# Four of eight gate/up pieces of each feed-forward chunk in seven block products instead of eight

## The chip, the cores and the metric

The kernel runs on one core of a Trainium2 chip. The metric is the device time of one execution in microseconds (us), from the runs shown; a profiled execution gives the span from its first to its last instruction. The engines are PE (TensorE: matmuls, with PEld for its weight loads), DVE (VectorE), ACT (ScalarE), POOL (GpSimd) and SP (SyncE, which here only issues loads). SBUF is the on-chip memory, PSUM holds matmul sums in eight banks of 128 x 512 fp32 numbers.

## What is computed

A two-layer decoder trunk on 256 tokens of width 2048 in fp32. Layer 0 mixes tokens by a diagonal state-space model with a GLU, layer 1 by sliding-window attention; each is followed by a SwiGLU feed-forward layer of inner width 5632, which is what the change touches:

```
D_MODEL = 2048; SEQ = 256; DEPTH = 2
D_FF = ((8 * D_MODEL // 3 + 255) // 256) * 256        # 5632

def swiglu(x, w_gate, w_up, w_down):
    return (jax.nn.silu(x @ w_gate) * (x @ w_up)) @ w_down

for i in range(DEPTH):
    hn = rmsnorm(h, norm_mix[i])
    ...
    h = h + mix
    hn = rmsnorm(h, norm_ffn[i])
    h = h + swiglu(hn, ffn_w_gate[i], ffn_w_up[i], ffn_w_down[i])
return rmsnorm(h, norm_final)
```

## The kernel before

**Numbers in two halves.** A big matrix product is made in three matmuls per block: each fp32 operand is split into a high half, rounded to the short form fp32r, and a low half, the rest, and the products high x high, high x low and low x high are summed in PSUM (`products`, lines 926 to 928). The activations are the stationary operand (128 x 128), the weights the moving one (128 x 512).

**Weight pieces.** All weights come as pieces of 512 x 512, in one list whose order is the order of use (class `Weights`). SP loads a piece (1 MB) into one of two `raw` buffers (`load`, line 109). ACT copies it into the high half of a tile `w` (`high`, line 122), DVE subtracts that from the raw piece for the low half (`low`, line 127). There are three `w` tiles. `next` (line 134) hands out piece i, splits up to piece i + 2 and loads up to i + 4; a `w` tile comes free when PE has done with the piece three before. A piece takes PE 4 row blocks x 2 token tiles x 3 = 24 matmuls (`piece`, line 930).

**A feed-forward layer** (`swiglu`, line 1128) works in eleven chunks of 512 inner columns. For a chunk, `gu` takes four gate pieces into two banks (one per tile of 128 tokens), four up pieces into two more, forms silu(gate) x up (lines 1152 and 1156), and turns the gated chunk around for use as stationary operand `hT`: 16 transposes of 32 x 256 on DVE (`blocks_turned`, line 1007), then the split by ACT and DVE (lines 1165 and 1166). The last chunk of a layer is turned by PE (line 1137). `down` multiplies `hT` with the down weights and adds to the residual `h` (line 1177), in four column blocks. The groups of chunks are `((0, 1, 2), (3, 4, 5), (6, 7, 8), (9, 10))`; the down product of a group comes after the first chunk of the next group (`ffn_order`, line 166). Four `hT` tiles (`b8`) exist.

**Small work in between.** Steps that turn and split are put into the list `left` and popped piece by piece in `linear` (line 941), so that they are written between the pieces' matmuls. In the norm ahead of a feed-forward layer (`Norm`, line 1010, with `blocks`) the residual is turned in the same way and split with the norm's weight as a scale (lines 1036 and 1037); the row scale of the norm is applied after the products. Another way of turning is used for the norm ahead of the attention (`through`): one DVE transpose of 32 x 32 blocks (line 1045), then POOL moves the blocks through DRAM (`through_dram`, lines 998 and 999), then the split (lines 1055 and 1060).

**Order.** The kernel is written in a tile language: it decides itself in which order ready instructions stand on an engine and puts in all waits; a tile of a pool with n buffers waits for the release of the one n before. Only where `keep_in_program_order` is used does the written order hold.

## Time and profile before

| | |
|---|---|
| time, median of 3 runs | 1981.72 us (1980.31 to 1982.71) |
| span of the profiled execution | 1976.9 us |
| HBM read / written | 363.72 MB / 8.91 MB |
| mean TensorE clock granted | 0.993 |
| pieces of weights | 332 (11 x 8 gate/up and 44 down pieces per feed-forward layer) |
| L926, L927, L928 with `xT`, `hT`, `gt` as stationary operand | 3 x 2528 matmuls, 390 ns each, overlapping |
| q1 (SP's loads) | 356.87 MB, 56.4% of 16 DMA engines |

The lines of the profile read: source line, engine, operation, tile written from tiles read, shapes and count, then the busy time in us, the mean duration in ns, and the idle time of the engine ahead of them with what ended it. In a timeline a line begins with the start and the duration in us, and ends with the idle time before it in brackets. In a table of stretches each engine has its busy time and the number of its instructions, in the order PE, PEld, DVE, ACT, POOL; then follow the granted clock, the share of the DMA engines' time and GB/s.

### The profile page before, as it was taken

The page shows a single profiled execution, that of the slowest core. Times are in us where ns is not written, and L with a number is a line of the kernel's source. Part 1 is how long each engine was busy: PE and PEld are TensorE (multiplying, and loading weights), DVE is VectorE, ACT ScalarE, POOL GpSimd, SP SyncE. Part 2 cuts the span into 40 slices and gives each one's busy share as a digit, 9 for nine tenths or more (in the row PEclk, how much of TensorE's full clock was granted, in tenths as well). Part 3 has the DMA queues.
Part 4 walks back from the last instruction along what each step waited for, and adds up shares of the span by engine and source line. Part 5 has one row for each costly group of instructions (what it writes and reads, how often), then busy time and mean ns, then how long its engine had stood idle before and what let it go on. Part 6 is the DMA issues. An engine that isn't in the chain of part 4 may idle for free.

```text
span 1976.9 us, 24861 instructions
## 1 busy us (share of the span) xinstructions
PE 1935.3 (98%) x10312; PEld 1600.9 (81%) x10312; DVE 1287.2 (65%) x1689; ACT 859.9 (43%) x839; POOL 130.5 (7%) x122
## 2 busy tenths in 40 slices
PE   8699999999999999999999999999999999999998
PEld 6578888888888888888888778888888888888886
DVE  8966667666556656665577888766654665566545
ACT  6554444343334333433455554443333434333333
POOL 6850000000000000000010110000000000000000
PEclk9899999999999999999999999999999999999999
DMA  4037666556666665656585864665566556656664
GB/s 131 24 103 224 209 207 199 182 186 209 192 192 188 195 197 186 201 189 205 176 280 186 261 226 150 195 209 192 191 192 192 191 191 201 195 190 188 205 191 149
DMA packets 188181, 374.23 MB, mean 189 GB/s; under 512 B 11203, under 2 KB 11267, under 8 KB 187941
## 3 DMA queue, kind: packets, MB, share of 16 engines
q1 hardware_dynamic: 183168, 356.87, 56.4%
q0 software_dynamic: 4064, 13.65, 2.1%
q10 hardware_dynamic: 836, 2.14, 0.3%
q8 instruction: 80, 1.31, 0.3%
q14 instruction: 33, 0.26, 0.0%
HBM read 363.72 MB, written 8.91 MB: 188 GB/s over the span
## 4 chain that ended last, share of the span: by engine, by line
PE 91%; DVE 6%; DMA 1%; issue 1%; ACT 1%; POOL 0%; DVEq 0%; POOLq 0%; ACTq 0%
PE acc L926 30%; PE acc L927 29%; PE acc L928 29%; DVE scan L577 1%; DVE V L582 1%; DVE V L580 1%; DVE w L127 1%; PE pv L214 1%; PE py L802 0%; DMA pT<-pd 0%; DMA pd<-bt 0%; PE px L214 0%; DVE bt L1285 0%; DMA raw<-in_attn_w_qkv_dram 0%; ACT w L122 0%
## 5 line engine op out<-in xcount | busy, mean ns | idle before, releaser
L127 DVE TENSOR_TENSOR w<-raw,w 128x2048 fp32r<-128x2048 f32 x330 | 756.9, 2294 | 579.4 <-ACT w L122 577.4
L122 ACT ACTIVATE w<-raw 128x2048 fp32r<-128x2048 f32 x332 | 636.1, 1916 | 840.6 <-PE acc L928 543.1
L926 PE MATMUL acc<-w,xT 128*128 128x512 f32 x1568 | 611.8, 390 | 0.0
L928 PE MATMUL acc<-w,xT 128*128 128x512 f32 x1568 | 611.0, 390 | 0.0
L927 PE MATMUL acc<-w,xT 128*128 128x512 f32 x1568 | 610.9, 390 | 0.0
L926 PEld LDWEIGHTS acc<-w,xT 128*128 128x128 f32 x1568 | 294.5, 188 | 62.4 <-issue 1.8
L928 PEld LDWEIGHTS acc<-w,xT 128*128 128x128 f32 x1568 | 294.5, 188 | 61.4 <-issue 0.3
L927 PEld LDWEIGHTS acc<-w,xT 128*128 128x128 f32 x1568 | 294.5, 188 | 60.7
L926 PE MATMUL acc<-w,hT 128*128 128x512 f32 x704 | 274.6, 390 | 0.0
L927 PE MATMUL acc<-w,hT 128*128 128x512 f32 x704 | 273.9, 390 | 0.0
L928 PE MATMUL acc<-w,hT 128*128 128x512 f32 x704 | 273.6, 390 | 0.0
L926 PEld LDWEIGHTS acc<-w,hT 128*128 128x128 f32 x704 | 132.2, 188 | 28.3 <-ACT hT L1139 1.2
L928 PEld LDWEIGHTS acc<-w,hT 128*128 128x128 f32 x704 | 132.2, 188 | 27.5
L927 PEld LDWEIGHTS acc<-w,hT 128*128 128x128 f32 x704 | 132.2, 188 | 27.2
L1007 DVE STREAM_TRANSPOSE bt<-act 32x256 f32<-32x256 f32 x320 | 139.6, 436 | 5.5
L927 PE MATMUL acc<-w,gt 128*128 128x512 f32 x256 | 99.9, 390 | 0.6 <-DVE w L127 0.6
L926 PE MATMUL acc<-w,gt 128*128 128x512 f32 x256 | 100.0, 391 | 0.0
L928 PE MATMUL acc<-w,gt 128*128 128x512 f32 x256 | 99.8, 390 | 0.0
L998 POOL DMA_DIRECT2D pd<-bt x40 | 21.9, 553 | 932.9 <-DVE bt L1045 842.7
L1165 ACT ACTIVATE hT<-bt 128x1024 fp32r<-128x1024 f32 x20 | 21.2, 1062 | 96.9 <-DVE bt L1007 96.8
L1007 DVE STREAM_TRANSPOSE bt<-h 32x256 f32<-32x256 f32 x128 | 55.8, 436 | 1.9
L1177 DVE TENSOR_TENSOR h<-h,acc 128x512 f32<-128x512 f32 x64 | 43.0, 686 | 21.4 <-PE acc L928 21.4
(249 smaller groups left out, 1283.3 us busy)
## 6 DMA issues: line engine op xcount, KB each, us to landing
raw<-in_ffn_w_gate_dram SPq DMA_DIRECT2D x88, 1024.0 KB, 5.2
raw<-in_ffn_w_up_dram SPq DMA_DIRECT2D x88, 1024.0 KB, 5.2
raw<-in_ffn_w_down_dram SPq DMA_DIRECT2D x88, 1024.0 KB, 5.1
raw<-in_s_w_glu_dram SPq DMA_DIRECT2D x32, 1024.0 KB, 5.4
raw<-in_attn_w_qkv_dram SPq DMA_DIRECT2D x20, 1024.0 KB, 5.2
raw<-in_attn_w_o_dram SPq DMA_DIRECT2D x16, 1024.0 KB, 5.2
pd<-bt POOLq DMA_DIRECT2D x24, 192.0 KB, 4.7
pT<-pd POOLq DMA_DIRECT2D x6, 768.0 KB, 5.8
```

The lines of the kernel that those rows point to most:

```text
L122: keep(S.activation(w[:, 0], self.raw[i], AF.Copy))
L127: keep(e.tensor_tensor(lo, self.raw[i], hi.bitcast(F32), op=ALU.subtract))
L214: return (lambda *a, **k: pin(f(*a, **k))) if self.on else f
L577: keep(V.tensor_tensor(t_, ws[..., part], bc(Vt[hf][:, k - 1, :, part], 1, 2), op=ALU.mult))
L580: V.tensor_tensor(v, v, t_[:, 0], op=ALU.add)
L926: keep(PE.matmul(acc, x_[:, 0], w[0][:, a], start=first, stop=False))
L927: PE.matmul(acc, x_[:, 0], w[1][:, a], start=False, stop=False)
L928: PE.matmul(acc, x_[:, 1], w[0][:, a], start=False, stop=last)
L998: nc.gpsimd.dma_start(d[t].rearrange("(q k) e -> k q e", q=4), v[32 * t : 32 * t + 32])
L1007: V.transpose(dst[32 * q : 32 * q + 32, :, :, 32 * tb : 32 * tb + 32], src[:, :, :, 32 * q : 32 * q + 32])
L1165: S.activation(o[:, 0], v, AF.Copy)
L1177: V.tensor_tensor(hc, hc, acc[t], op=ALU.add)
```

## The change

**Seven products.** Of the eight gate/up pieces of a chunk four (`SEVEN`) are made by Strassen's scheme in Winograd's form. A gate/up piece is now 256 rows of the up and the gate weights side by side, 2 x 2 blocks of 128 x 512: two row blocks by up/gate. The activations' counterpart is 2 x 2 blocks, two token tiles by the same two row blocks. The eight block products of such a pair become seven, of sums and differences of blocks. The products of all four pieces are summed in seven banks, and the four results are put together from them at the end of the last (`sums`, and the additions of `c11` to `c22`). The other four pieces are made in eight products as before, into the same banks and an eighth, `c22`.

**Forms of the operands.** `sevenths` makes a weight piece ready: DVE forms four differences `f` from the raw piece, ACT and DVE split them into the tile `w`, and split the three blocks used as they are into a second tile `d`, of which there is one. `forms` does the same for the activations of two of the four row blocks in a norm chunk.

**Order.** The chunks are in groups of two (the last of three), and half of the previous group's down pieces follow each chunk from the third on. The gated chunk is turned through DRAM (`moved`) instead of by 16 DVE transposes; the last chunk too. The first six down pieces of the last group use the first two chunks of it first (`LAST_ORDER`). The last part of the attention's output product is moved out of the attention's pool, so that the new tiles can have its space.

```diff
-FF_GROUPS = ((0, 1, 2), (3, 4, 5), (6, 7, 8), (9, 10))
+FF_GROUPS = ((0, 1), (2, 3), (4, 5), (6, 7), (8, 9, 10))
+SEVEN = (0, 2, 4, 6)
...
-                nc.sync.dma_start(t, self.src[i].rearrange("(a p) n -> p a n", p=P))
+                aps, _ = self.src[i]
+                t = pp.tile([P, 4, 512], F32, tag="raw", name=nm("raw"), bufs=2)
+                v = t.rearrange("p (k s) n -> p s k n", s=len(aps))
+                for s, ap in enumerate(aps):
+                    nc.sync.dma_start(v[:, s], ap.rearrange("(a p) n -> p a n", p=P))
...
+        def sevenths(self, i):
+            self.load(i + 1)
+            r = self.raw[i]
+            w = self.place(i)
+            d = self.pool.tile([P, 2, 3, 512], F32R, tag="sd", name=nm("sd"), bufs=1)
+            f = self.pool.tile([P, 4, 512], F32, tag="sf", name=nm("sf"), bufs=1)
+            V.tensor_tensor(f[:, 0:2], bc(r[:, 0], 1, 2), r[:, 1:3], op=ALU.subtract)
+            V.tensor_tensor(f[:, 2], r[:, 2], f[:, 0], op=ALU.subtract)
+            V.tensor_tensor(f[:, 3], r[:, 3], f[:, 2], op=ALU.subtract)
+            S.activation(w[:, 0], f, AF.Copy)
+            S.activation(d[:, 0], r[:, 1:4], AF.Copy)
+            V.tensor_tensor(w[:, 1], f, w[:, 0].bitcast(F32), op=ALU.subtract)
+            V.tensor_tensor(d[:, 1], r[:, 1:4], d[:, 0].bitcast(F32), op=ALU.subtract)
+            pairs = [(d[:, 0, j], d[:, 1, j]) for j in range(3)] + [(w[:, 0, j], w[:, 1, j]) for j in range(4)]
+            self.hl.append(dict(zip(("b11", "b22", "b21", "t1", "t3", "t2", "t4"), pairs)))
...
+    LAST_ORDER = [(n, c) for cs in (FF_GROUPS[-1][:-1], FF_GROUPS[-1][-1:]) for n in (0, 1) for c in cs]
...
+            for p in range(8):
+                W.add(*(w[i, 256 * p : 256 * (p + 1), 512 * c : 512 * (c + 1)] for w in (w_up, w_gate)),
+                      seven=p in SEVEN)
...
+    def ffn_order(gu, down, last):
         for g, chunks in enumerate(FF_GROUPS):
-            for n, c in enumerate(chunks):
+            for j, c in enumerate(chunks):
                 gu(c)
-                if n == 0 and g > 0:
-                    down(g - 1)
-        down(len(FF_GROUPS) - 1)
+                if g > 0 and j < 2:
+                    down(g - 1, (2 * j, 2 * j + 1))
+        last()
...
+    def moved(src):
+        v, land = block_tile(), wp.tile([P, 2, 512], F32, tag="act", name=nm("act"), bufs=2)
+        V.transpose(v.rearrange("p a t -> p (a t)").rearrange("p (q t a k) -> p t a q k", q=4, t=2, a=4),
+                    src.rearrange("p t (a q k) -> p t a q k", a=4, q=4))
+        through_dram(land.rearrange("p t c -> p (t c)").rearrange("p (b e) -> p b e", b=4),
+                     v.rearrange("p a t -> p (a t)").rearrange("p (q e) -> p q e", q=4))
...
+        def forms(self, n, o, v):
+            gc = gcol[:, self.g, 4 * n : 4 * n + 4]
+            g0, g1 = gc[:, 0:1], gc[:, 1:2]
+            hi = o[:, 1024:1920].rearrange("p (f t) -> p f t", f=7)
+            lo = W.pool.tile([P, 7, P], F32R, tag="xs", name=nm("xs"), bufs=4)
+            f = W.pool.tile([P, 7, P], F32, tag="xf", name=nm("xf"), bufs=1)
+            S.activation(f[:, 0], v[:, 0, :P], AF.Copy, scale=g0)
+            S.activation(f[:, 1:3].rearrange("p f t -> p (f t)"), v[:, 1], AF.Copy, scale=g1)
+            V.scalar_tensor_tensor(f[:, 3], v[:, 0, P:], g0, f[:, 2], ALU.mult, ALU.add)
+            V.scalar_tensor_tensor(f[:, 5], v[:, 0, P:], g0, f[:, 0], ALU.mult, ALU.subtract)
+            V.tensor_tensor(f[:, 4], f[:, 3], f[:, 0], op=ALU.subtract)
+            V.tensor_tensor(f[:, 6], f[:, 1], f[:, 4], op=ALU.subtract)
+            S.activation(hi, f, AF.Copy)
+            V.tensor_tensor(lo, f, hi.bitcast(F32), op=ALU.subtract)
+            names = ("a11", "a12", "a22", "s1", "s2", "s3", "s4")
...
+        def three(acc, x_, w, first, last):
+            PE.matmul(acc, x_[0], w[0], start=first, stop=False)
+            PE.matmul(acc, x_[0], w[1], start=False, stop=False)
+            PE.matmul(acc, x_[1], w[0], start=False, stop=last)
+
+        M = {"m1": ("a11", "b11"), "c11": ("a12", "b21"), "c12": ("s4", "b22"), "c21": ("a22", "t4"),
+             "m5": ("s1", "t1"), "m6": ("s2", "t2"), "m7": ("s3", "t3")}
+        FIRST = ("m1", "m6", "m7", "m5", "c11", "c21", "c12")
+        REST = ("m1", "c11", "c12", "m5", "m7", "m6", "c21")
+
+        def gu(c):
+            acc = {}
+            u = W.pool.tile([P, 4, 512], F32, tag="u", name=nm("u"), bufs=1)
+
+            def sums():
+                S.copy(u[:, 0], acc["m1"])
+                V.tensor_tensor(u[:, 1], u[:, 0], acc["m6"], op=ALU.add)
+                V.tensor_tensor(u[:, 2], u[:, 1], acc["m7"], op=ALU.add)
+                V.tensor_tensor(u[:, 1], u[:, 1], acc["m5"], op=ALU.add)
+                V.tensor_tensor(u[:, 3], u[:, 2], acc["m5"], op=ALU.add)
+
+            for p in range(8):
+                w = W.next()
+                forms, e = norm.xt[p // 2]
+                if p in SEVEN:
+                    for m in FIRST if p == 0 else REST:
+                        if p == 0:
+                            acc[m] = bank([P, 512], "acc")
+                        x_, b = M[m]
+                        three(acc[m], forms[x_], w[b], p == 0, m[0] == "m" and p == SEVEN[-1])
+                else:
...
+                if p == SEVEN[-1]:
+                    sums()
+                pop_left((6 if c == 0 else 7) - p)
+            if c == 0:
+                r[0] = norm.scale()
+            sg = wp.tile([P, 2, 512], F32, tag="act", name=nm("act"), bufs=2)
+            for t, (g, m) in enumerate(((0, "c11"), (2, "c21"))):
+                V.tensor_tensor(u[:, g], u[:, g], acc[m], op=ALU.add)
+                S.activation(sg[:, t], u[:, g], AF.Silu, scale=r[0][:, t : t + 1])
+            for t, (g, m) in enumerate(((1, "c12"), (3, "c22"))):
+                V.tensor_tensor(u[:, g], u[:, g], acc[m], op=ALU.add)
+                V.scalar_tensor_tensor(sg[:, t], u[:, g], r[0][:, t : t + 1], sg[:, t], ALU.mult, ALU.mult)
             o = turned_tile("hT")
+            ht[c] = o
+
+            def send():
+                lv = moved(sg)
+
+                def split():
+                    for t in range(2):
+                        hi, lo = (o[:, i, :, t * P : t * P + P].rearrange("p a (b k) -> p a b k", b=4)
+                                  for i in range(2))
+                        v = lv[:, :, t].rearrange("p b a k -> p a b k")
+                        S.activation(hi, v, AF.Copy)
+                        V.tensor_tensor(lo, v, hi.bitcast(F32), op=ALU.subtract)
+
+                left.extend([lambda: None] * 2 + [split])
+
+            left.append(send)
...
+        def last():
+            accs = [[bank([P, 512], "acc") for _ in range(2)] for _ in range(2)]
+            for i, (n, c) in enumerate(LAST_ORDER):
+                piece(accs[n], ht[c], c == FF_GROUPS[-1][0], c == FF_GROUPS[-1][-1])
+                pop_left(3 - i)
+            for n in range(2):
+                add(n, accs[n], True)
+            down(len(FF_GROUPS) - 1, (2, 3))
```

In what the diff leaves out, the pieces that are not in `SEVEN` run as two row blocks x (gate, up) x two token tiles, three matmuls each, into `c11`, `c21`, `c12` and `c22`; `add` adds a bank to the residual and, in the last group, hands it to the next norm; and the new tiles (`sd`, `sf`, `xs`, `xf`, `u`) lie in a pool of their own, which is open during the two feed-forward layers.

More of the change, by code (lines that the diff above doesn't have):

```diff
@@ L1126, in glu, with pop_left @@
                 norm.chunk(c, t)
+    def pop_left(pieces):
+        for _ in range(-(-len(left) // max(1, pieces))):
+            left.pop(0)()
     def swiglu(norm, out_norm):
@@ new lines, in add, with down, last @@
+        def add(n, acc, done):
+            for t in range(2):
+                hc = h[:, n, t]
+                V.tensor_tensor(hc, hc, acc[t], op=ALU.add)
+                if done:
+                    out_norm.chunk(n, t)
+        def down(g, ns):
+            xt = Later(ht, FF_GROUPS[g])
+            end = g == len(FF_GROUPS) - 1
+            for n in ns:
+                add(n, linear(xt, len(FF_GROUPS[g]), halves=end and out_norm.g is None and n == NCH - 1), end)
+        def last():
+            accs = [[bank([P, 512], "acc") for _ in range(2)] for _ in range(2)]
[4 more added lines that the diff above has]
+                add(n, accs[n], True)
+            down(len(FF_GROUPS) - 1, (2, 3))
@@ L1183 @@
+        ffn_order(gu, down, last)
     class Later:
```

137 lines of the change are left out of this document (52 added, 85 removed).

## The prediction

> **What bounds the kernel now.** I read the page first, then the waits, the stretches of the two feed-forward layers, and the timeline of ACT and DVE inside one.
>
> ```profile
> span 1976.9 us, 24861 instructions
> PE 1935.3 (98%) x10312; PEld 1600.9 (81%) x10312; DVE 1287.2 (65%) x1689; ACT 859.9 (43%) x839; POOL 130.5 (7%) x122
> PE 91%; DVE 6%; DMA 1%; issue 1%; ACT 1%; POOL 0%; DVEq 0%; POOLq 0%; ACTq 0%
> 277.00:1000.00 723.00, 723.00 (x3194) 598.63 (x3193) 434.12 (x386) 289.42 (x189) 5.16 (x9) 1.00 0.61 194
> 723.73 1.92 ACT L122 ACTIVATE w<-raw 128x2048 fp32r<-128x2048 f32 x1 [3.52 <-PE acc L928]
> 729.17 1.92 ACT L122 ACTIVATE w<-raw 128x2048 fp32r<-128x2048 f32 x1 [3.52 <-DVE h L1177]
> 725.68 2.29 DVE L127 TENSOR_TENSOR w<-raw,w 128x2048 fp32r<-128x2048 f32 x1 [3.15 <-ACT w L122]
> ```
>
> PE is busy in 98% of the span and holds 91% of the chain. In the first feed-forward layer it is busy for all 723 us, at clock 1.00, with DVE busy 434 us (60%). ACT's high half of a weight piece starts every 5.44 us, when PE frees a weight tile: 5.44 / 24 matmuls = 0.2267 us per matmul. So a matmul removed there is worth 0.2267 us, provided weights stay ready. DVE has 3.15 us idle per piece: that is the reserve which the change spends.
>
> **Removed.** Four pieces of a chunk go from 24 to 21 matmuls: 12 per chunk, 22 chunks, 264 x 0.2267 = 59.9 us. The last chunk of each layer also loses its eight PE transposes, 2 x 0.88 = 1.8 us.
>
> ```profile
> 1928.66 0.88 PE tr L1137 x8
> L127 DVE TENSOR_TENSOR w<-raw,w 128x2048 fp32r<-128x2048 f32 x330 | 756.9, 2294 | 579.4 <-ACT w L122 577.4
> L1276 DVE TENSOR_TENSOR sc<-sc,sm 128x1024 f32<-128x1024 f32 x8 | 9.8, 1219 | 0.0
> L1276 DVE TENSOR_TENSOR sc<-sc,sm 128x512 f32<-128x512 f32 x8 | 5.5, 688 | 0.1
> L1166 DVE TENSOR_TENSOR hT<-bt,hT 128x1024 fp32r<-128x1024 f32 x20 | 24.5, 1225 | 20.3 <-ACT hT L1165 20.3
> L1165 ACT ACTIVATE hT<-bt 128x1024 fp32r<-128x1024 f32 x20 | 21.2, 1062 | 96.9 <-DVE bt L1007 96.8
> L1177 DVE TENSOR_TENSOR h<-h,acc 128x512 f32<-128x512 f32 x64 | 43.0, 686 | 21.4 <-PE acc L928 21.4
> L1156 DVE SCALAR_TENSOR_TENSOR act<-acc,ry,act 128x512 f32<-128x512 f32 x44 | 31.5, 750 | 10.9 <-PE acc L928 10.9
> L1045 DVE STREAM_TRANSPOSE bt<-h 128x1024 f32<-128x1024 f32 x4 | 5.0, 1242 | 0.1
> L1007 DVE STREAM_TRANSPOSE bt<-act 32x256 f32<-32x256 f32 x320 | 139.6, 436 | 5.5
> ```
>
> **DVE per piece.** A seven-product piece has the differences f (1024 + 512 + 512 elements: 1.22 + 0.69 + 0.69 = 2.60 us), the low half of w (2.29) and that of d (1536 elements). No row has 1536; it lies between 1.23 (1024) and 2.29 (2048), and I take the middle, 1.76. Together 6.65 us against 2.29 now; on 88 pieces +384 us. ACT adds the high half of d, between 1.06 and 1.92, middle 1.49.
>
> **DVE per chunk.** Gate/up: 4 x 6.65 + 4 x 2.29 + eight sums of products at 0.69 + two products at 0.75 + one whole transpose 1.24 (in place of 16 at 0.436) + two low halves of hT at 0.69 = 45.4 us. PE needs 180 x 0.2267 = 40.8. The four down pieces that follow most chunks: DVE 4 x 2.29 + 4 x 0.69 = 11.9, PE 21.8. Chunk and down pieces together: DVE 57.4, PE 62.6 (92%). So DVE fits where chunk and down alternate, and doesn't in the first three chunks of a layer, where only after the third the first down pieces come.
>
> **Head of each layer.** From its first piece to its first down piece PE needs 3 x 40.8 = 122.4 us. DVE has to do, by then: the first chunk's pieces 2 to 7 (3 x 8.94 = 26.8), two chunks (2 x 35.8 = 71.6), two down pieces 4.6, sums and products 7.0 + 7.0 + 2.8, two hT 5.2, and what the norm leaves over:
>
> ```profile
> 1234.35 4.47 DVE L1007 STREAM_TRANSPOSE bt<-h 32x256 f32<-32x256 f32 x10
> 1241.17 2.70 DVE L1007 STREAM_TRANSPOSE bt<-h 32x256 f32<-32x256 f32 x6
> L1037 DVE SCALAR_TENSOR_TENSOR xT<-bt,gcol,xT 128x256 fp32r<-128x256 f32 x32 | 13.4, 480 | 0.2 <-ACT xT L1036 0.2
> L1060 DVE SCALAR_TENSOR_TENSOR xT<-act,gcol,xT 128x128 fp32r<-128x128 f32 x32 | 8.7, 347 | 0.0
> ```
>
> 16 transposes (7.2 here), the new forms (four of 128 columns at up to 0.35, one of 896 at under 1.22, two of 256 at 0.48: 3.5) and some 2 us of residual adds and scale. Sum 137.7, 15 over. The f of piece 2 (2.6) can be done before, the second down piece (2.3) later: 10 us if DVE never idles. With 1 us idle in each of eleven pairs (next part) it is 21. I take 12, near the first, since DVE's work is ready far more often than not: 24 us for two layers. The second layer's head starts behind a stretch in which DVE has no reserve at all:
>
> ```profile
> 250.00:300.00 50.00, 50.00 (x222) 41.43 (x221) 35.41 (x42) 24.16 (x26) 0.00 (x0) 1.00 0.61 200
> 1200.00:1250.00 50.00, 50.00 (x222) 41.44 (x221) 48.30 (x74) 26.15 (x33) 0.00 (x0) 1.00 0.53 173
> ```
>
> DVE is busy 48.3 of 50 us, PE never waits. Here fall the first seven-product piece (+4.4) and the forms of two chunks (each 3.5 in place of 4 x 0.48, +3.2 together): 0 to 7.6 us; I take the middle, 4, as nothing tells how far DVE is ahead there. Before the first layer it has some 14 us of reserve in 50, and I count nothing.
>
> **The pair.** A seven-product piece and a plain one take PE 21 + 24 matmuls, 10.2 us. There are two raw buffers, so the seven-product piece always has the same one.
>
> ```profile
> SPq L109 <- DVE w L127: 1564.1, 316, 43.9
> raw<-in_ffn_w_gate_dram SPq DMA_DIRECT2D x88, 1024.0 KB, 5.2
> 773.47 1.78 DVE L1007 STREAM_TRANSPOSE bt<-act 32x256 f32<-32x256 f32 x4
> 775.29 2.29 DVE L127 TENSOR_TENSOR w<-raw,w 128x2048 fp32r<-128x2048 f32 x1
> 777.61 4.03 DVE L1007 STREAM_TRANSPOSE bt<-act 32x256 f32<-32x256 f32 x9
> 781.67 2.29 DVE L127 TENSOR_TENSOR w<-raw,w 128x2048 fp32r<-128x2048 f32 x1
> ```
>
> SP issues a load when DVE's low half has freed its buffer. Now a buffer's round is 5.2 (load) + 1.92 + 2.29 = 9.4 of 10.9 us. After, it is load 5.2 + f 2.60 + low of d 1.76 = 9.6 of 10.2, **if** d's halves come before w's: d needs only the raw piece, so ACT can split it while DVE makes f. As written, w's low half stands first, and the round is 5.2 + 2.60 + 1.92 + 2.29 + 1.76 = 13.8. The four rows show that DVE's order isn't the written one (eight transposes after each piece's split), but filled by what is ready; by that I expect d first. Two loads of 512 KB in place of one cost a second issue on SP, which has nothing else there; I take 5.2 for both, not below, and up to 0.5 more, which brings the round to 10.1. The single d tile: after the chunk's first piece, whose b blocks PE uses to its end, ACT and DVE need 1.49 + 1.76 of the plain piece's 5.44 us. It fits with 2.2 to spare, which a waiting hT split (1.4) can take. So a chunk that follows down pieces costs from 0 to 1.5; I take 0.5, as the round fits: 16 x 0.5 = 8 us.
>
> **Banks.** A chunk holds all eight. The next one's first products (12 matmuls, 2.7 us) use the four that the sums freed during the last plain piece; then c11 and c21 wait for DVE's adds, 0.7 us apart, behind a low half of 2.29. This sits inside the 12 us of the head; before down pieces only two banks are wanted.
>
> **hT through DRAM.** DVE's transpose, POOL's five DMAs and ACT's split:
>
> ```profile
> 1008.58 1.24 DVE L1045 STREAM_TRANSPOSE bt<-h 128x1024 f32<-128x1024 f32 x1
> 1010.11 2.19 POOL L998 DMA_DIRECT2D pd<-bt x4 [8.08 <-DVE bt L1045]
> 1015.89 0.76 POOL L999 DMA_DIRECT2D act<-pd  x1 [3.59 <-ACT w L122]
> 1021.20 1.69 ACT L1055 ACTIVATE xT<-act,gcol 128x256 fp32r<-128x256 f32 x4
> ```
>
> 12.6 us from transpose to split. Pairs give every hT a whole chunk to come back, except the last: sums and products end some 3.5 us after PE, one low half 2.3 may go first, then 12.6 and 2.1 for the split: 20.5 against 4 x 5.44 = 21.8 of down pieces on the other two chunks. Hidden with 1.3 to spare; if a load delays it, 0 to 3. I take 1 per layer: 2 us. POOL is idle in the layer otherwise (5.2 us of 723). The round trip adds about 1 MB to the 12 MB of a chunk and its down pieces, on DMA engines busy at 0.61; I count no more than the 0.5 above for it.
>
> **Sum.** 1976.9 - 59.9 - 1.8 + 24 + 4 + 8 + 2 = 1953.2. The median of the runs shown is 1981.72, 4.8 above the span; so **1958**. Costs at both ends (head 10 to 21 per layer, before the second 0 to 7.6, chunk 0 to 1.5, last 0 to 3) give 20 to 80 us of stall: 1940 to 2000; with the head half hidden, since the sum of DVE's work there is an estimate, 1930.
>
> **Rivals.**
> 1. *Raw held too long* (slower). If w's low half is put before d's, the round is 13.8: PE waits 3.6 in each pair, three pairs in 16 chunks and four in 6: 72 x 3.6 = 259. With the 61.7 gained and the last chunk's 2: 2181; in half of the pairs, 2050. For it: the written order, and d's tile being free only 2 us into the piece, when w may already be ready. Against: the rows above. It decides from the point where the raw buffer's round grows by more than 0.6 us, from 9.6 past the pair's 10.2.
> 2. *DVE pays its excess in every chunk.* Weights are split at most two pieces ahead, so the reserve in the down pieces may not reach the chunk: 22 x (45.4 - 40.8) = 101, with 61.7 gained: 2021, slower. At 60% of it the gain is just given back: 1981, no change.
> 3. *The clock.* Behind PE's longest wait the same six matmuls took twice as long as later:
>
> ```profile
> 91.53 2.93 PE L758 MATMUL pm<-k,shift 128*128 128x256 f32 x6 [14.22 <-ACT k L751]
> 95.10 1.54 PE L758 MATMUL pm<-k,shift 128*128 128x256 f32 x6
> ```
>
> If a head's 12 us came as three waits, each followed by about 3.4 us at half speed, 6 x 1.7 = 10 us more: 1968. That is a rule of the Trainium skill, "TensorE: Matmul & The Clock Gate", Part 1: a window of some 3.4 us without work halves the clock until a busy one has passed. By the two rows the trace agrees after 14 us; no wait here shows where it begins.
>
> Against the change also speaks the Trainium skill, "Perfetto Trace Analysis", Identifying the Most-Contended Engine: the same gap repeating on the engine that should be full can mean too few buffers for the next tile. PE here shows no such gap yet; by it the pattern would be rival 1 or 2.
>
> 4. *The change doesn't do what it says*: no sign; the new matmuls have the same shape, and each product again takes three to a bank.
>
> **Chances.** Forecast 0.64 (own range 1930 to 1977; all upper ends at once are counted with rival 2); rival 1 0.14; rival 2 0.11 in full and 0.08 with the gain given back; rival 3 0.03, faster too. A measurement here tells about 0.2% (4 us). Faster 0.67, within 0.2% 0.08, slower 0.25. The range reaches into rivals 2 and 1 until some 0.15 is left out above, and 0.03 below: 1925 to 2035.
>
> **What would show it.** PE's matmuls fall by 264 and 16; DVE's busy time grows by the 384 us of the pieces and 22 x 8 x 0.69 = 121 of the sums, less 112 for the transposes, to near 1680 us (86%); in the timeline d's low half ahead of w's, and SP's loads for seven-product pieces 9.6 to 10.2 us apart; PE's waits on DVE in the first three chunks, some 12 us per layer, and hardly any later. Waits of 3 us in every pair would mean rival 1, waits at each chunk's end rival 2, a granted clock below 1.00 in the layers rival 3.

## The result, and the profile after

The changed kernel takes **2012.65 us** (median of four runs, 2006.47 to 2016.69) beside 1981.43 (median of four, one more than stands above; 1980.31 to 1982.71) for the kernel before on the same chip: ratio **1.0159, 95% interval 1.0138 to 1.0181**. It is slower by 31 us; 24 us faster was forecast. The profiled run's span is 2014.7 us, 37.8 above that of before.

From the page of the changed kernel: the span, the engines' busy times, the chain's shares, and the two groups to look at (busy, mean of one in ns | idle time ahead of them, and what ended it):

```profile
span 2014.7 us, 25452 instructions
PE 1923.9 (95%) x10032; PEld 1547.5 (77%) x10032; DVE 1648.1 (82%) x1979; ACT 1001.6 (50%) x977; POOL 197.4 (10%) x232
PE 47%; DVE 26%; ACT 10%; issue 8%; DMA 8%; POOL 0%; SPq 0%; ACTq 0%; DVEq 0%; POOLq 0%
...
L142 DVE TENSOR_TENSOR w<-sf,w 128x2048 fp32r<-128x2048 f32 x88 | 201.6, 2291 | 139.7 <-ACT w L140 139.4
L140 ACT ACTIVATE w<-sf 128x2048 fp32r<-128x2048 f32 x88 | 168.5, 1914 | 257.0 <-DVE sf L139 257.0
```

The 280 PE instructions are gone (10312 to 10032) and VectorE's busy time, 1648 us, is near the 1680 forecast. But PE's share of the chain fell from 91% to 47%, and VectorE, the engine with the new work, stands idle for 139 us in front of w's low half (L142), 1.6 us in each of the 88 pieces: it waits for ScalarE's w high half (L140), which in turn waited for f (L139).

The stretches of the changed kernel: two in the head of the first layer, two in that of the second, one among chunks and down pieces (columns: stretch, length, busy time of PE, PEld, DVE, ACT, POOL with instructions, granted clock, DMA share, GB/s):

```profile
327.00:377.00 50.00, 46.78 (x196) 35.86 (x195) 44.69 (x43) 28.05 (x23) 3.14 (x5) 1.00 0.58 192
377.00:427.00 50.00, 43.62 (x177) 33.60 (x177) 42.60 (x37) 23.06 (x17) 2.96 (x5) 0.97 0.56 185
1277.00:1327.00 50.00, 44.41 (x182) 34.60 (x181) 48.03 (x59) 27.16 (x23) 0.00 (x0) 0.97 0.50 167
1327.00:1377.00 50.00, 44.68 (x178) 34.16 (x178) 45.11 (x42) 24.99 (x19) 2.95 (x5) 0.94 0.64 211
600.00:665.00 65.00, 64.74 (x281) 52.02 (x280) 54.66 (x45) 32.16 (x22) 2.95 (x5) 1.00 0.63 210
```

In the heads PE misses 3 to 6 us of every 50, and in three of the four stretches the granted clock is below 1.00. Among chunks and down pieces PE seems full, since the end of a matmul is modelled; its instructions per time tell more. So I counted in the trace how long each block of matmuls took from start to start, less its number of 512-column matmuls times the 0.2267 us of the undisturbed spacing. What is over is called stall here. The same was done for the profiled execution of every run below (us; "16 chunks" are the fourth to eleventh chunk of both layers; "half clock" is how many matmuls start 0.40 to 0.46 us after the one before, three or more in a row, and their excess, which is part of the other columns and of attention):

| run | median | heads A, B | 16 chunks | last chunk A, B | half clock |
|---|---|---|---|---|---|
| before | 1981.4 | 0, 0 | 0 | 1.3, 1.3 | 0 |
| **after** | 2012.7 | 21.3, 32.9 | 35.6 | 5.7, 1.0 | 50: 10.0 |
| e1 VectorE's order pinned | 1996.9 | 13.0, 21.7 | 39.0 | 0.9, 1.9 | 16: 3.2 |
| e2 no seven products | 1985.8 | 1.3, 1.5 | 6.8 | 0, 0 | 0 |
| e3 from the fourth chunk on | 1962.2 | 1.3, 1.5 | 26.0 | 1.2, 0.6 | 0 |
| e4 e3 with e1's pins | 1975.1 | 1.3, 1.4 | 32.8 | 7.2, 3.7 | 20: 4.0 |
| **e5 both orders pinned** | 1969.4 | 13.0, 21.6 | 7.5 | 2.9, 1.7 | 18: 3.6 |
| e6 e3 with e5's pins | 1952.4 | 1.3, 1.5 | 7.2 | 6.5, 2.0 | 6: 1.2 |
| e7 e5, VectorE 61 us more | 1994.5 | 18.3, 30.7 | 17.2 | 6.8, 5.7 | 66: 13.2 |
| e8 e5, GpSimd helps in heads | 1998.6 | 27.9, 38.0 | 7.3 | 4.7, 6.0 | 61: 12.2 |
| e9 e5, no low half of d in heads | 1950.6 | 6.2, 13.1 | 9.4 | 2.8, 3.9 | 17: 3.4 |
| e10 e6, set-up behind hT | 1947.2 | 1.3, 1.5 | 6.9 | 4.1, 0.2 | 7: 1.4 |

For after, with attention's 3.5 us (43.0 of excess, 39.5 before), the stalls are 54.2 + 35.6 + 6.7 + 3.5 = 100.0 us. Less the 59.9 us of matmuls and the 2.5 that the last chunks lost before, 37.6 are left of the 37.8 between the spans. A profiled execution need not lie at the median: that of the changed kernel is its slowest run, that of e5 its fastest (1962.74), so their spans are 53.7 us apart and their medians 43.3.

Where the 35.6 us of the 16 chunks come from is seen on VectorE. Its timeline over a seven-product and a plain piece of the changed kernel (start, length, line, names, idle time before and its releaser):

```profile
606.34 1.22 DVE L137 TENSOR_TENSOR sf<-raw 128x1024 f32<-128x1024 f32 x1
...
616.95 1.22 DVE L137 TENSOR_TENSOR sf<-raw 128x1024 f32<-128x1024 f32 x1
618.09 1.75 DVE L143 TENSOR_TENSOR sd<-raw,sd 128x1536 fp32r<-128x1536 f32 x1
619.75 0.68 DVE L138 TENSOR_TENSOR sf<-raw,sf 128x512 f32<-128x512 f32 x1
620.47 0.69 DVE L139 TENSOR_TENSOR sf<-raw,sf 128x512 f32<-128x512 f32 x1
623.15 2.29 DVE L142 TENSOR_TENSOR w<-sf,w 128x2048 fp32r<-128x2048 f32 x1 [1.99 <-ACT w L140]
625.36 2.29 DVE L128 TENSOR_TENSOR w<-raw,w 128x2048 fp32r<-128x2048 f32 x1
```

The low half of d (L143) stands **inside** f, between its first instruction (L137) and its second (L138). So f ends 1.7 us later, ScalarE's w high half starts later by as much, and VectorE has nothing left to do while it runs: 1.99 us idle. From one L137 to the next the round is 10.61 us; PE needs 45 x 0.2267 = 10.2. Every later pair of a chunk stalls for 0.4 to 0.6 us, and the first piece of a chunk, where the second product already wants w's low half, for up to 2.1. In 64 of the 88 seven-product pieces d's low half has this place; in 20 it stands between f's second and third instruction, in 3 behind f, and in one behind w's low half.

### The profile page after: what moved, and what is told of

It is laid out like the page before. It is cut to its first block, busy times and chain, and to the rows that moved or that the text cites. A ratio compares the mean times of both kernels' runs of the same rounds, so it can differ in the third digit from the quotient of the medians.

```text
span 2014.7 us, 25452 instructions
## 1 busy us (share of the span) xinstructions
PE 1923.9 (95%) x10032; PEld 1547.5 (77%) x10032; DVE 1648.1 (82%) x1979; ACT 1001.6 (50%) x977; POOL 197.4 (10%) x232
## 4 chain that ended last, share of the span: by engine, by line
PE 47%; DVE 26%; ACT 10%; issue 8%; DMA 8%; POOL 0%; SPq 0%; ACTq 0%; DVEq 0%; POOLq 0%
PE acc L954 9%; PE acc L956 9%; PE acc L955 9%; DVE w L128 6%; PE acc L1184 6%; PE acc L1183 6%; PE acc L1185 6%; DVE sd L143 5%; DMA raw<-in_ffn_w_down_dram 4%; ACT w L140 4%; ACT w L123 3%; DMA raw<-in_ffn_w_gate_dram 3%; DVE sf L137 2%; ACT sd L141 2%; DVE sf L139 2%
## 5 line engine op out<-in xcount | busy, mean ns | idle before, releaser
L128 DVE TENSOR_TENSOR w<-raw,w 128x2048 fp32r<-128x2048 f32 x242 | 554.4, 2291 | 136.2 <-ACT w L123 134.2
L123 ACT ACTIVATE w<-raw 128x2048 fp32r<-128x2048 f32 x244 | 466.9, 1914 | 351.8 <-DMA raw<-in_ffn_w_down_dram 143.7
L1184 PE MATMUL acc<-w,xT 128*128 128x512 f32 x1056 | 418.9, 397 | 14.8 <-DVE w L142 13.9
L1183 PE MATMUL acc<-w,xT 128*128 128x512 f32 x1056 | 370.3, 401 | 23.4 <-ACT w L140 11.8
L142 DVE TENSOR_TENSOR w<-sf,w 128x2048 fp32r<-128x2048 f32 x88 | 201.6, 2291 | 139.7 <-ACT w L140 139.4
L140 ACT ACTIVATE w<-sf 128x2048 fp32r<-128x2048 f32 x88 | 168.5, 1914 | 257.0 <-DVE sf L139 257.0
L1185 PE MATMUL acc<-w,xT 128*128 128x512 f32 x704 | 273.9, 390 | 0.0
L1183 PEld LDWEIGHTS acc<-w,xT 128*128 128x128 f32 x1056 | 194.5, 190 | 91.9 <-ACT w L123 35.3
L1184 PEld LDWEIGHTS acc<-w,xT 128*128 128x128 f32 x1056 | 200.0, 189 | 72.8 <-DVE w L142 21.9
L141 ACT ACTIVATE sd<-raw 128x1536 fp32r<-128x1536 f32 x88 | 131.3, 1492 | 198.5 <-DMA raw<-in_ffn_w_gate_dram 114.9
L143 DVE TENSOR_TENSOR sd<-raw,sd 128x1536 fp32r<-128x1536 f32 x88 | 154.4, 1754 | 10.6 <-ACT sd L141 10.4
L1185 PEld LDWEIGHTS acc<-w,xT 128*128 128x128 f32 x704 | 132.5, 188 | 26.4
L1185 PE MATMUL acc<-w,xs 128*128 128x512 f32 x352 | 140.2, 399 | 0.0
L137 DVE TENSOR_TENSOR sf<-raw 128x1024 f32<-128x1024 f32 x88 | 107.4, 1220 | 2.0 <-DMA raw<-in_ffn_w_gate_dram 1.8
```

The lines of the kernel that those rows point to most:

```text
L123: keep(S.activation(w[:, 0], self.raw[i], AF.Copy))
L128: keep(e.tensor_tensor(lo, self.raw[i], hi.bitcast(F32), op=ALU.subtract))
L140: S.activation(w[:, 0], f, AF.Copy)
L141: S.activation(d[:, 0], r[:, 1:4], AF.Copy)
L142: V.tensor_tensor(w[:, 1], f, w[:, 0].bitcast(F32), op=ALU.subtract)
L143: V.tensor_tensor(d[:, 1], r[:, 1:4], d[:, 0].bitcast(F32), op=ALU.subtract)
```

## Experiments

Theory A: it is the **order** of the instructions on VectorE (and ScalarE), not their sum. Theory B, the prediction's second rival: VectorE has **too much work**, in every chunk.

### e1 to e4: order, the seven products themselves, the heads

e1 pins VectorE's order as f, d's low half, w's low half. `keep_in_program_order` puts an instruction behind the one written before it on its engine.

```diff
-            V.tensor_tensor(w[:, 1], f, w[:, 0].bitcast(F32), op=ALU.subtract)
-            V.tensor_tensor(d[:, 1], r[:, 1:4], d[:, 0].bitcast(F32), op=ALU.subtract)
+            keep = tc.keep_in_program_order
+            keep(V.tensor_tensor(d[:, 1], r[:, 1:4], d[:, 0].bitcast(F32), op=ALU.subtract))
+            keep(V.tensor_tensor(w[:, 1], f, w[:, 0].bitcast(F32), op=ALU.subtract))
```

> The change as it is, but VectorE's work for a seven-product piece is pinned in the order f (three instructions), d's low half, w's low half; in the changed kernel d's low half stands between f's first and second instruction, so that ScalarE gets w's f late and VectorE idles 2.0 us per pair of pieces ahead of w's low half. Theory A (order: the round of a pair is 10.6 us on VectorE because of this idle time, where TensorE needs 10.2): the idle time ahead of w's low half falls from 2.0 to about 0.2 us, the stalls of the 16 chunks behind down pieces fall from 2.2 us to 0.5 or less (27 us), the heads lose some 10 us of their 54: 1975 us (1965 to 1985). Theory B (load: VectorE simply has too much work in every chunk): its busy time is as before, so is the time: 2012 us, within 6.

e2 and e3 choose the seven-product pieces by chunk. A piece that takes all eight products in a block with forms needs the quadrant a21 as well; it becomes an eighth form (and the forms are built in `u`'s buffer, not in one of their own). A chunk without seven-product pieces has no sums; its four totals go straight from the banks to the gate.

```diff
-SEVEN = (0, 2, 4, 6)
+def seven(c):
+    return ()                                # e2
+    return (0, 2, 4, 6) if c > 2 else ()     # e3
...
-                      seven=p in SEVEN)
+                      seven=p in seven(c))
...
-            lo = W.pool.tile([P, 7, P], F32R, tag="xs", name=nm("xs"), bufs=4)
+            lo = W.pool.tile([P, 8, P], F32R, tag="xs", name=nm("xs"), bufs=4)
...
+            S.activation(f[:, 7], v[:, 0, P:], AF.Copy, scale=g0)
```

> The whole change but for the seven products: every piece takes all eight block products, chunks still in pairs, gated chunks through DRAM, down pieces in two halves, loads in two pieces of 512 KB; nothing is left out of the result. Theory A and B alike (the rest of the change costs little, what is lost is lost to the preparation of the seven-product pieces): 1981 to 1990 us, the upper end if layer A's last chunk (5.7 us) and attention (3.5 us) lose as much as in the changed kernel. A rival (the new order of the chunks and the way through DRAM cost the time themselves): 2010 us or more, since 59.9 us of matmuls come back.

> The change with seven products only from the fourth chunk of each layer on; the first three take all eight. 6 chunks x 12 matmuls x 0.2267 = 16 us of matmuls come back, the 54 us that the heads lost should go. If the heads' loss belongs to the heads (no down pieces beside them, VectorE full): 2012 - 54 + 16 = 1975 us (1968 to 1982). If it is a debt that the first chunks with seven products pay wherever they stand: the fourth to sixth chunk pay it instead, 2015 us or a little less.

e4 has both edits, e1's and e3's.

> Both edits: seven products from the fourth chunk on, and VectorE's order pinned as f, d's low half, w's low half. Theory A: 1975 - 27 = 1948 us (1940 to 1958), faster than both kernels. Theory B: as without the pinned order, 1975 us.

Measured (each ratio is to runs of the kernel before made alongside, with medians of 1979.2 to 1980.2): e1 1996.94 (ratio 1.0083, 1.0065 to 1.0100), e2 1985.81 (1.0029, 1.0018 to 1.0040), e3 1962.16 (0.9911, 0.9896 to 0.9926), e4 1975.06 (0.9970, 0.9960 to 0.9981).

**e2** clears the rest of the change: the order of the chunks, the way through DRAM and the two loads cost 5.7 us (3.6 to 7.9 by the interval). By the table it is 9.6 us, less the 2.5 that the last chunks lost before: the 7.1 between the profiled spans (1984.0 and 1976.9). The 9.6 are 0.11 us in every second piece, the one whose stationaries come from the new tiles: its 24 matmuls follow each other 4.6 ns later on average. Why they do wasn't tried. The seven products bring 59.9 us less matmul work and cost 59.9 + 2012.7 - 1985.8 = 87 us.

**e3** shows that the heads' loss belongs to the heads: it doesn't wander to the fourth chunk (1.5 and 2.1 us there), and the kernel is faster than both, and below the 1968 to 1982 expected. One thing didn't fit: the code of the 16 chunks is unchanged, yet they lose 26.0 in place of 35.6, and in other places. Nothing there was pinned, and behind other heads the scheduler settled on another mixture: in some pieces d's low half behind f, in others inside it, and ahead of the first piece of some chunks the plain piece's two halves before w's, where PE loses up to 4.1 us. d's low half still stands inside f in 48 of the 64 pieces, but behind a loss ahead of the first piece most later pairs lose only the 0.09 us of the spacing. So it is order again, but the place of d's low half alone doesn't say at which piece PE loses.

**e1 and e4** missed: e1 lies between what A and B expected, e4 at B's 1975. e1's heads fell from 54 to 35, more than expected, but the 16 chunks lost 39.0, and e4 is slower than e3. With VectorE pinned, the stall moved. In e1, on VectorE:

```profile
1551.27 0.69 DVE L139 TENSOR_TENSOR sf<-raw,sf 128x512 f32<-128x512 f32 x1
1555.40 1.76 DVE L143 TENSOR_TENSOR sd<-raw,sd 128x1536 fp32r<-128x1536 f32 x1 [3.44 <-ACT sd L141]
```

and on ScalarE of the same run:

```profile
1552.08 1.92 ACT L140 ACTIVATE w<-sf 128x2048 fp32r<-128x2048 f32 x1 [4.70 <-DVE sf L139]
1553.90 1.47 ACT L141 ACTIVATE sd<-raw 128x1536 fp32r<-128x1536 f32 x1
```

and on PE:

```profile
1555.42 0.49 PE L1184 MATMUL acc<-sd,xT 128*128 128x512 f32 x1
1557.21 0.50 PE L1185 MATMUL acc<-sd,xT 128*128 128x512 f32 x1 [1.30 <-DVE sd L143]
```

Now it is ScalarE that takes w's high half (L140) before d's (L141), although d's needs only the raw piece. VectorE, which must do d's low half first, waits 3.4 us, and PE 1.3 us for it. So pinning VectorE's order alone didn't help here, where two engines hand work to and fro. Pinning ScalarE's alone wasn't tried.

### e5 to e8: both engines pinned, and VectorE's load changed

e5 writes ScalarE's two high halves in the order d, w and pins them too:

```diff
-            S.activation(w[:, 0], f, AF.Copy)
             S.activation(d[:, 0], r[:, 1:4], AF.Copy)
+            keep(S.activation(w[:, 0], f, AF.Copy))
```

> As the run with VectorE's order pinned (1997 us), and ScalarE's pinned too: d's high half, then w's. In that run ScalarE has w's high half ahead of d's in the third piece of nearly every chunk behind down pieces, and TensorE waits 1.9 us there for d's low half. Theory A (order): the stalls of those 16 chunks fall from 39 us together to some 8 (0.41 each is the slower spacing of the matmuls with the new stationaries), the heads stay at about 35: 1966 us (1958 to 1975). Theory B (VectorE's load, in every chunk): the stalls move again and stay, 1997 us.

> Seven products from the fourth chunk on, with the same two engines' orders pinned. Theory A: the 26 us that the 16 chunks lose in the run without pins fall to 8: 1944 us (1938 to 1950). Theory B: 1962 us as without.

e7 and e8 start from e5:

```diff
             keep(V.tensor_tensor(w[:, 1], f, w[:, 0].bitcast(F32), op=ALU.subtract))
+            keep(V.tensor_tensor(f[:, 0], f[:, 0], f[:, 1], op=ALU.add))     # e7
...
-                      seven=p in SEVEN)
+                      seven=(1 + (c < 3)) * (p in SEVEN))                    # e8
...
-            keep(V.tensor_tensor(w[:, 1], f, w[:, 0].bitcast(F32), op=ALU.subtract))
+            e = PL if self.src[i][1] == 2 else V
+            keep(e.tensor_tensor(w[:, 1], f, w[:, 0].bitcast(F32), op=ALU.subtract))
```

> As the kernel with both orders pinned, and VectorE does one more sum of 128x512 (0.69 us) behind w's low half of every seven-product piece, 88 in all, 61 us of work. If VectorE's load is the bound in the heads alone: behind down pieces 4 x 0.69 = 2.8 us a chunk go into its 5 us of spare time and cost nothing, in the heads 24 x 0.69 = 16.6 us are paid: 10 to 20 us more than without. If its load is the bound in all chunks: 45 to 61 us more. If only the chain of one piece (f, w's high half, w's low half) is: 0 to 4 us more.

> As the kernel with both orders pinned, but w's low half of the 24 seven-product pieces in the first three chunks of each layer is worked out by GpSimd (4.6 us by the two such instructions in the trace, 2.3 on VectorE), which takes 9.2 us a chunk off VectorE. If VectorE's load bounds the heads: their stalls fall from about 35 us to 10 or less, 20 to 30 us less than without. If the chain f, w's high half, w's low half bounds them: it gets 2.3 us longer, 0 to 20 us more. If GpSimd slows VectorE down beside it, VectorE's instructions there last longer than in the other run.

Measured: e5 **1969.38** (0.9943, 0.9924 to 0.9962), e6 1952.44 (0.9872, 0.9849 to 0.9895), e7 1994.47 (1.0075, 1.0060 to 1.0090), e8 1998.63 (1.0095, 1.0078 to 1.0112).

**e5 settles the 16 chunks.** The same instructions with the same work in another order, and the change is 43 us faster and on the other side of the kernel before. The 16 chunks lose 7.5 us: 0.41 in 14 of them, where e2, without seven products, has 0.42 of slower spacing. The same group on e5's page (w's low half is L144 there) and VectorE's timeline:

```profile
L144 DVE TENSOR_TENSOR w<-sf,w 128x2048 fp32r<-128x2048 f32 x88 | 201.6, 2291 | 22.6 <-ACT w L142 22.1
```

```profile
653.26 1.23 DVE L137 TENSOR_TENSOR sf<-raw 128x1024 f32<-128x1024 f32 x1 [0.57 <-DMA raw<-in_ffn_w_gate_dram]
654.52 0.69 DVE L138 TENSOR_TENSOR sf<-raw,sf 128x512 f32<-128x512 f32 x1
655.25 0.69 DVE L139 TENSOR_TENSOR sf<-raw,sf 128x512 f32<-128x512 f32 x1
655.86 1.75 DVE L143 TENSOR_TENSOR sd<-raw,sd 128x1536 fp32r<-128x1536 f32 x1
657.92 2.29 DVE L144 TENSOR_TENSOR w<-sf,w 128x2048 fp32r<-128x2048 f32 x1 [0.31 <-ACT w L142]
```

The idle time ahead of w's low half fell from 139.7 to 22.6 us; d's low half now fills the time in which ScalarE makes w's high half. VectorE's busy time is no less (1659.7 us against 1648.1), so theory B falls for these chunks. e6, without the heads' products, missed its 1944 by 8 us, of which 5.3 are layer A's last chunk (6.5, in e3 1.2; below).

**e7 and the heads.** Stretches of e5, one in the second layer's head and one among chunks and down pieces:

```profile
1277.00:1377.00 100.00, 93.83 (x392) 74.47 (x393) 94.36 (x89) 54.69 (x41) 5.88 (x10) 0.97 0.60 202
700.00:800.00 100.00, 100.00 (x439) 82.29 (x439) 86.56 (x70) 51.42 (x35) 2.94 (x5) 1.00 0.62 210
```

In the head VectorE is busy for 94 of 100 us and PE waits; later VectorE has 13 us to spare and PE doesn't wait. With the additional sums the heads lose 49.0 in place of 34.6, 14.4 us more for 16.6 us of new work; 6.0 of the 14.4 are more matmuls at half clock behind the longer waits. The 16 chunks lose 9.7 more for 44 us of it, so the spare time there is not quite free to use: it shows in the chunks' first pieces, 0.6 us each. The last chunks lose 12.5 in place of 4.6, which I didn't follow up. Together this is the 32 us between the two profiled spans (1993.2 and 1961.0; the medians differ by 25, where 10 to 20 was expected), and 9.6 of it are half clock, inside these sums.

**e8** was meant to take work off VectorE in the heads, and they got worse, 65.9 in place of 34.6. In the first layer's head (277 to 430 us) of e8 the groups of w's low half on GpSimd and of the plain pieces' low half on VectorE are

```profile
L145 POOL TENSOR_TENSOR w<-sf,w 128x2048 fp32r<-128x2048 f32 x11 | 53.2, 4835 | 223.0 <-issue 172.4 <-ACT w L142 50.6
L128 DVE TENSOR_TENSOR w<-raw,w 128x2048 fp32r<-128x2048 f32 x13 | 47.2, 3631 | 22.5 <-ACT w L123 22.5
```

and in e5, same stretch:

```profile
L128 DVE TENSOR_TENSOR w<-raw,w 128x2048 fp32r<-128x2048 f32 x14 | 32.0, 2287 | 5.0 <-ACT w L123 4.8
```

VectorE's subtraction takes 3.63 us on average where it took 2.29. This is the last case that the expectation names. So e8 can't tell what bounds the heads: GpSimd takes w's low half off VectorE, but needs 4.83 us for it, and VectorE's other low halves last longer beside it.

### e9 and e10: less work in the heads, and the last chunk

e9 repeats e8's question without a second engine: e5, and in the first three chunks no low half of d. The kernel leaves that part of the result out: the products take d's high half a second time, so that PE has as many matmuls.

```diff
-                      seven=p in SEVEN)
+                      seven=(1 + (c < 3)) * (p in SEVEN))
...
+            head = self.src[i][1] == 2
+            if not head:
-            keep(V.tensor_tensor(d[:, 1], r[:, 1:4], d[:, 0].bitcast(F32), op=ALU.subtract))
+                keep(V.tensor_tensor(d[:, 1], r[:, 1:4], d[:, 0].bitcast(F32), op=ALU.subtract))
...
-            pairs = [(d[:, 0, j], d[:, 1, j]) for j in range(3)] + ...
+            pairs = [(d[:, 0, j], d[:, 0 if head else 1, j]) for j in range(3)] + ...
```

> As the kernel with both orders pinned (1969 us), but d's low half of the 24 seven-product pieces in the first three chunks of each layer isn't worked out; the products take d's high half in its place, so that the matmuls are as many as before and the result is off by that part. VectorE loses 4 x 1.75 = 7.0 us a chunk there, 42 in all, and no other engine gets work. If VectorE's load bounds the heads (45.4 against TensorE's 40.8 us a chunk): their stalls fall from 34.6 us to 12 or less, 1942 to 1952 us. If what bounds them is the chain f, w's high half, w's low half, or the loads: it is 1.7 us shorter a piece at most, and they stay above 25 us: 1960 us or more.

e10 is e6 with attention's set-up on GpSimd put behind the transfers of the last gated chunk:

```diff
-            PL.iota(ji[:, 0:128], pattern=[[1, 128]], base=0, channel_multiplier=-1)
+            tc.keep_in_program_order(PL.iota(ji[:, 0:128], pattern=[[1, 128]], base=0, channel_multiplier=-1))
...
-            nc.gpsimd.dma_start(sk, sinks[0].unsqueeze(0).to_broadcast([P, HEADS]))
+            tc.keep_in_program_order(nc.gpsimd.dma_start(sk, sinks[0].unsqueeze(0).to_broadcast([P, HEADS])))
```

> Seven products from the fourth chunk on, both orders pinned (1952 us), and attention's set-up on GpSimd (two iotas, the sinks' load) pinned behind the transfers of the last gated chunk and of attention's input. In the run without this the set-up stands ahead of the last chunk's four transfers to DRAM, which start at 940.8 us though their source was written at 938.4, and TensorE waits 4.6 us for hT behind it, with a window of half clock after it (2.0 us). If the set-up is what makes hT late: layer A's last pieces lose 2 to 3 us in place of 6.5, 1948 us. If the set-up is then late for the scores: 1952 us or more.

Measured: e9 1950.55 (0.9852, 0.9835 to 0.9868), e10 **1947.23** (0.9834, 0.9819 to 0.9848).

**e9**: the time is inside the band expected of a load-bound head, 18.8 us below e5 by the medians and 10.9 by the profiled spans. But the heads lose 19.3 us in place of 34.6, neither the 12 or less of a load-bound head nor the 25 or more of the other case. Together with e7 this says: VectorE's load costs PE time in the heads, about half of what they lose, and other things the rest. 2.8 of the 19.3 are the slower spacing that e2 has in the heads. The largest rest is the first piece of layer B, 6.8 us here and 6.7 to 8.9 in every run with seven products there. On e5's VectorE, ahead of it:

```profile
1227.95 2.29 DVE L128 TENSOR_TENSOR w<-raw,w 128x2048 fp32r<-128x2048 f32 x1
1230.28 3.59 DVE L1045 STREAM_TRANSPOSE bt<-h 32x256 f32<-32x256 f32 x8
1233.90 1.23 DVE L137 TENSOR_TENSOR sf<-raw 128x1024 f32<-128x1024 f32 x1
```

The raw piece had landed by 1229.55 (ScalarE starts on d there), but f has to wait behind eight block transposes of h. That this order is the cause wasn't tried.

**e10**: the last chunk of layer A in e6, on GpSimd (five of its nine rows):

```profile
935.24 0.23 POOL L1298 IOTA ji<- 128x128 int32 x1 [53.48 <-DVE act L1244]
...
936.36 1.30 POOL L1301 CAST nd<-ji 128x384 f32<-128x384 int32 x1
...
938.45 2.43 POOL L1306 TENSOR_SCALAR_AFFINE_SELECT nd<-nd 128x256 f32<-128x256 f32 x1
940.83 2.19 POOL L1028 DMA_DIRECT2D pd<-bt  x4
950.31 0.77 POOL L1029 DMA_DIRECT2D act<-pd  x1 [7.28 <-DMA pd<-bt]
```

and in e10:

```profile
937.61 2.18 POOL L1028 DMA_DIRECT2D pd<-bt  x4 [53.82 <-DVE bt L1034]
945.99 0.76 POOL L1029 DMA_DIRECT2D act<-pd  x1 [6.20 <-DMA pd<-bt]
```

The four transfers that turn hT start 3.2 us earlier; 1.1 of that is VectorE's transpose, which also ends earlier there (937.31 against 938.45), the rest the set-up. Layer A's last chunk loses 4.1 us in place of 6.5, where 2 to 3 was expected, so the set-up is not all that makes hT late. The profiled spans differ by 3.6 us (the medians by 5), and 1.8 of it is layer B's last chunk, which has no such set-up and lost 0.2 in place of 2.0; that the edit did this isn't shown. e10 is the fastest of all: seven products only where down pieces stand beside them, the two orders pinned, and the set-up out of hT's way: 1.7% below the kernel before.

## Why the prediction was wrong

**The step that failed** stands in "The pair": "The four rows show that DVE's order isn't the written one [...], but filled by what is ready; by that I expect d first." It asked whether d's low half comes before or after *w's*, and priced both (9.6 and 13.8 us a round). VectorE's order indeed wasn't the written one, d's low half did come before w's, and rival 1 with its 13.8 us didn't occur (w's low half comes first in one piece of 88). But "filled by what is ready" has a third place for it: d's high half is ready as soon as the piece has landed, so d's low half slipped in ahead of f's second part. The check also looked at one loop only, the raw buffer's. The loop that closed at 10.61 us runs over two engines, f, ScalarE's w high half, w's low half, the plain piece's low half, next f, and had 1.99 us of waiting in it that no sum of busy times shows.

By terms (us; forecast, after, and e5, which has the order that the forecast assumed):

| term | forecast | after | e5 |
|---|---|---|---|
| matmuls and PE transposes removed | -61.7 | -62.4 | -62.4 |
| heads, with the way into layer B | 24 + 4 | 54.2 | 34.6 |
| 16 chunks after down pieces | 8 | 35.6 | 7.5 |
| last chunks | 2 | 6.7 | 4.6 |
| attention | 0 | 3.5 | -0.3 |
| sum | -23.7 | +37.6 | -16.0 |

- **Attention** lost 3.5 us that weren't forecast, 1.4 of them one window of half clock; they are gone in e5, and I didn't follow them up.
- **Removed work and durations** were right: 264 matmuls fewer at 0.2267 us each and the 16 PE transposes, d's low half 1.754 us (1.76 estimated), its high half 1.492 (1.49).
- **16 chunks**: 8 us were forecast for waits in the raw buffer's round; with the order assumed (e5) they lose 7.5, with the order that came 35.6. The 28 us between are the largest part of the miss. That 8 and 7.5 agree is luck: 0.41 of e5's 0.47 a chunk is the slower spacing, which wasn't forecast, and 0.9 us in all are left for the wait that was.
- **Heads**: 28 forecast, 54.2 found. 20 of the 26 went with the order (e5). The other 6.6 are size: the first piece of layer B lost 6.9 us, where 4 was taken from 0 to 7.6, and e5's two windows of half clock, 3.6 us, both fall into that head. Of e5's 34.6, 2.8 are the slower spacing, so the waits that were forecast are smaller by as much.
- **Banks** cost nothing behind down pieces, as forecast: in e5 a chunk's first piece loses 0.11 us in 14 of 16, which is the spacing. In the heads, where the forecast put their cost inside the 12 us, they do cost: the second and third chunk of both layers wait 1.1 to 1.5 us for VectorE's additions (L1230) to free a bank, 5.0 us together. One of the four, on e5's PE:

```profile
343.81 0.50 PE L1184 MATMUL acc<-sd,xT 128*128 128x512 f32 x1 [1.47 <-DVE u L1230]
```

- **hT through DRAM** was right for every chunk but the last. There 1.3 us of slack was forecast. In the changed kernel PE waited 3.3 us, and a window of half clock behind it took 1.7. What wasn't counted is GpSimd's set-up for attention, which becomes ready at that moment and stands in the queue ahead of hT's transfers: in e6 they start 2.4 us behind the end of VectorE's transpose, in e10 0.3. How much it was in the changed kernel wasn't tried.
- **Rival 2** (2021 us) came nearest in time and in sight, stalls in every chunk, but not as mechanism: VectorE's load costs PE much in the heads alone (e7, e9). In the 16 chunks the same load in another order stalls 0.9 us beside the spacing (e5).
- **Rival 3**, the clock, was given 0.03 and happened beside the main cause: 50 matmuls at half clock in seven windows, 10.0 us (and the runs of this kernel spread over 10 us, those of before over 2.4). That the rival's sum is 10 us too is chance: two of the seven windows lie outside the heads. It came with the stalls: with the order mended 3.6 us were left.
- The rule cited against the change (Trainium skill, "Perfetto Trace Analysis", Optimization Strategy: a gap that repeats can mean too few buffers) pointed at the right sign, the same 0.4 to 0.6 us in every later pair, but no buffer was short: e5 has as many as the changed kernel. Here the repeating gap was a loop longer than PE's own round, and its cause the order.

## What to carry to other kernels

A busy sum that fits (57.4 of 62.6 us here) says only that the work could fit. Where two engines hand a piece to and fro, write out the loop with every wait in it, for each order in which ready instructions can fall, and pin the order on **both** engines; pinning one moved the stall here. And apply a scheme that trades one engine's work for another's only in the stretches where the second engine has spare time beside it: without the heads the same scheme went from +1.6% to -0.9%, with the orders pinned and hT's transfers first to -1.7%.

## What was not expected of the hardware

**The clock falls after waits shorter than thought.** PE of the changed kernel in the first layer's head:

```profile
386.43 0.40 PE L1185 MATMUL acc<-sd,xs 128*128 128x512 f32 x1
387.70 0.73 PE L1183 MATMUL acc<-w,xT 128*128 128x512 f32 x2 [0.87 <-ACT w L140]
390.75 0.50 PE L1184 MATMUL acc<-w,xT 128*128 128x512 f32 x1 [2.33 <-DVE w L142]
391.09 0.44 PE L1185 MATMUL acc<-w,xs 128*128 128x512 f32 x1
391.33 0.63 PE L1184 MATMUL acc<-w,xT 128*128 128x512 f32 x1
391.75 0.63 PE L1185 MATMUL acc<-w,xs 128*128 128x512 f32 x1
392.18 0.63 PE L1183 MATMUL acc<-w,xT 128*128 128x512 f32 x1
```

Two waits of 0.87 and 2.33 us with two matmuls between them, and from 391.3 on the matmuls start 0.43 us apart in place of 0.23. The Trainium skill ("TensorE: Matmul & The Clock Gate", Part 1) speaks of a free-running window of some 3.4 us that is idle; here no stretch of 3.4 us was wholly idle. Single waits do it too: two of the seven windows stand behind one wait of 3.17 and of 3.69 us, and in e8 one of 2.67 us was enough:

```profile
345.96 0.80 PE L1186 MATMUL acc<-w,xT 128*128 128x512 f32 x1 [2.67 <-POOL w L145]
346.56 0.63 PE L1187 MATMUL acc<-w,xs 128*128 128x512 f32 x1
346.98 0.63 PE L1185 MATMUL acc<-w,xT 128*128 128x512 f32 x1
```

On the other side a wait of 2.64 us in e1 (3.04 from one matmul to the next at 908.3) was followed by none at half clock. What decides between them no run here shows. So a short wait of PE can cost a second time, here 1.0 to 2.2 us for each of the seven windows (5 to 11 matmuls at 0.2 more).

**GpSimd blocks VectorE.** In e8, VectorE:

```profile
343.23 4.83 DVE L128 TENSOR_TENSOR w<-raw,w 128x2048 fp32r<-128x2048 f32 x1
```

and GpSimd:

```profile
341.34 4.57 POOL L145 TENSOR_TENSOR w<-sf,w 128x2048 fp32r<-128x2048 f32 x1 [7.30 <-ACT w L142]
```

GpSimd's instruction ends at 345.91; VectorE's, begun at 343.23, ends at 348.06, 2.15 us after that. That fits an instruction that waited and then ran nearly at its own length (2.29). The Trainium skill ("SBUF — State Buffer", Who interferes with whom) states it: a VectorE instruction with two inputs in SBUF contends with a GpSimd instruction that reads SBUF, and the later one blocks. The trace agrees. The low halves are all such subtractions, and in e8 GpSimd was no help with them beside VectorE.
